# Attention's eight query tiles paired 7,4 / 6,5 / 3,0 / 2,1, with the second tile's masked row copied to free room

## The chip, the cores and the metric

The kernel runs on one core of a Trainium2 chip. The core has five engines with queues of their own: TensorE (PE in the profile; its weight loads are PEld), VectorE (DVE), ScalarE (ACT), GpSimd (POOL) and SyncE (SP), which here only starts DMA transfers. The metric is the device time of one execution in microseconds (us). The kernel before takes 1288.67 us, the median of three runs (1285.36 to 1290.3).

## The reference

One layer with two branches. All of it is computed in float32:

```
h = RMSNorm(x);  h @ w_in -> z_ssm | xBC | dt | q | k | v | f | z_att | g_ssm | g_att
A: causal conv on xBC, SiLU, chunked SSD scan, gated group RMSNorm
B: 16 heads of 64; F = cumsum(log sigmoid(f))
   logits[t, s] = q[t].k[s] / 8 + F[t] - F[s]   for s <= t
   o = softmax(logits) @ v, in blocks of 128 queries;  y_att = o * silu(z_att)
out = (sigmoid(g_ssm) * (A @ w_branch_ssm) + sigmoid(g_att) * (B @ w_branch_att)) @ w_out
x + RMSNorm(out)
```

There are 1024 positions and 1024 channels, so attention has eight query tiles of 128 rows, 0 to 7. Tile i needs the keys 0 to 128(i+1), and only its last 128 keys, the diagonal block, need the causal mask.

## The kernel before, in words

The large products (the projection, both branch products, the last product) run as a stream of matmuls with 512 columns. They are written as fast products of 2x2 blocks, and each operand as a high and a low part, so each step of the stream also needs VectorE and ScalarE work: `sum` (sums of weight blocks), `wop` (high and low part of a weight), `s` and `th` (products taken out of PSUM). `Stream.half()` issues half a step: six matmuls and the work around them.

Attention lies inside this stream. A head pair `hp` (two heads, `e` = 0 and 1) is worked through in six groups; the loop index is m = 6 hp + g. A group is a pair of query tiles against one half `h` of the keys (keys 512 to 1023 are half 1). For each m the order is:

1. `scores` for the pair's first tile (u = 0) and then its second (u = 1): for each head three matmuls into a PSUM tile `s`. VectorE adds the row `fb` (F of the keys, with a large number added on the diagonal block where the mask lies) and takes the minimum in the same operation (L1494), then reads the minimum out into `nm`. ScalarE takes the exponential in place in `ex` and sums it (L1505).
2. `weighted`: the product of the probabilities of the group before with the values, into the PSUM tile `av`.
3. `ahead` halves of the stream (`stream.halves(ahead)`).
4. `loads(m)`: transfers and masks for later groups; then `turned`: TensorE turns `ex` in blocks of 128 x 128 into PSUM tiles `pt` (their buffers are those of `s`, four in all), and ScalarE (L1544), or VectorE for one block of four in the first six head pairs (L1542), copies them to `p`.
5. `behind` halves of the stream.

`room(m)` splits the stream's halves over the groups by the shares in `rooms`; with three halves for a group two go ahead and one behind, with four it is two and two. Operations wrapped in `pin` keep their written order on their engine; the others are placed between them by a planner that plays the program through with its own costs and puts high-priority operations first.

The score rows have these widths (in columns), per head:

| group | tiles, half of the keys | width of u = 0, u = 1 |
|---|---|---|
| 0 | (7,6), 1 | 512, 384 |
| 1 | (7,6), 0 | 512, 512 |
| 2 | (5,4), 1 | 256, 128 |
| 3 | (5,4), 0 | 512, 512 |
| 4 | (3,2), 0 | 512, 384 |
| 5 | (1,0), 0 | 256, 128 |

The mask. `fb` is one row of F, the same on all 128 partitions, and both tiles of a pair read the same 512 columns of it. GpSimd adds `far` (the triangle) to the diagonal block of the first tile in place (`mask(hp, i)`). The second tile's diagonal block must stay unmasked there, because the first tile reads it as ordinary keys. So GpSimd writes the second tile's masked 128 columns to `spare`, the last 128 columns of `ex` at u = 1, which no second tile of a diagonal group uses. The second tile's score row then takes two VectorE operations: the unmasked columns with `fb` (L1494, minimum into `na`), and the diagonal columns with `spare` (L1501), which starts from `na` and gives `nm`. Where the row is only its diagonal block (tiles 4 and 0), it is the second operation alone.

GpSimd runs in written order: the masks, the differences for later products (L211), and transfers it starts itself (L193, L645, L1072, L1575).

## Time and profile before

| | |
|---|---|
| median of three runs | 1288.67 us |
| the profiled execution, its own time | 1288.65 us |
| its span, first to last instruction | 1286.6 us |
| mean granted TensorE clock | 0.994 of full speed |
| TensorE busy | 1246.2 us (97%) |
| VectorE busy | 1015.6 us (79%) |
| ScalarE busy | 790.0 us (61%) |
| GpSimd busy | 329.5 us (26%) |

The profiled execution spends 2.05 us outside the span. Times below are in us from the start of the span. Attention lies between about 680 and 1130. In a row of the timeline the columns are start, duration (of the whole run of instructions, where there are several), engine, line, operation, output and inputs, shape, count, and in square brackets the idle time before it with what ended it. In a row of groups, the numbers after the bar are the busy time in us and the mean of one in ns, and then the idle time of the engine before them. In a row of windows, the columns are the window, its length, the busy time of PE, PEld, DVE, ACT and POOL with instruction counts, the granted clock, the DMA share and GB/s.

### The profile page before, as it was taken

Reading aid. Unit: us, or ns where it says so; the run is one execution under the profiler, and the core shown is the slowest. Engines: PE = TensorE matmul, PEld = TensorE weight load, DVE = VectorE, ACT = ScalarE, POOL = GpSimd, SP = SyncE. Lnnn points to the kernel's source line nnn. Section 1 sums busy time; section 2 is a strip of 40 time slices with the busy share of each in tenths; the row PEclk is TensorE's granted clock in tenths of the full one; section 3 lists DMA queues with packets and bytes.
Section 4 is the critical chain, followed back from the end, with each engine's and each line's share of the span. In section 5 each row is a group of like instructions: output and inputs, shape, how many; then the busy total and the mean of one; then the engine's idle time right before and its main releaser. Section 6 shows DMA issues by size and latency. Waiting matters only on the chain.

```text
span 1286.6 us, 20828 instructions
## 1 busy us (share of the span) xinstructions
PE 1246.2 (97%) x6800; PEld 984.9 (77%) x6800; DVE 1015.6 (79%) x2053; ACT 790.0 (61%) x1719; POOL 329.5 (26%) x384
## 2 busy tenths in 40 slices
PE   5999999999999999999999999999989999999998
PEld 3688888888888888888887777777767776678886
DVE  7999876987789878987667776776779677797975
ACT  7745665566665665576546665667767666743754
POOL 4000440014300340124011322423122222347052
PEclk9999999999999999999999999999989999999999
DMA  8232543545345533653384665576777656756932
GB/s 297 70 123 70 165 147 98 189 156 178 128 147 179 184 126 117 196 180 123 107 290 136 213 213 185 200 239 206 245 284 219 206 196 230 238 185 217 367 113 101
DMA packets 152236, 233.56 MB, mean 182 GB/s; under 512 B 15200, under 2 KB 60736, under 8 KB 152128
## 3 DMA queue, kind: packets, MB, share of 16 engines
q1 hardware_dynamic: 136064, 196.08, 47.3%
q10 hardware_dynamic: 10560, 18.06, 3.7%
q0 software_dynamic: 5504, 18.09, 3.7%
q8 instruction: 53, 0.87, 0.3%
q14 instruction: 55, 0.45, 0.1%
HBM read 162.99 MB, written 72.34 MB: 183 GB/s over the span
## 4 chain that ended last, share of the span: by engine, by line
PE 80%; DVE 8%; DMA 4%; ACT 4%; issue 3%; SPq 1%; POOL 0%; DVEq 0%; ACTq 0%; POOLq 0%
PE pb L128 34%; PE pc L128 20%; PE pd L128 6%; PE pt L131 5%; PE av L128 4%; PE s L128 4%; PE yps L128 2%; DVE wop L351 1%; DMA raw<-in_wu 1%; PE st L128 1%; DVE ex L1494 1%; DMA xt<-in_x 1%; PE tr L131 1%; ACT wop L350 1%; PE tr_v L131 1%
## 5 line engine op out<-in xcount | busy, mean ns | idle before, releaser
L351 DVE TENSOR_TENSOR wop<-sum,wop 128x512 fp32r<-128x512 f32 x180 | 140.6, 783 | 51.5 <-ACT wop L350 50.7
L350 ACT ACTIVATE wop<-sum 128x512 fp32r<-128x512 f32 x180 | 112.3, 626 | 100.9 <-DVE sum L356 48.5
L1505 ACT ACTIVATE ex<-ex,nm 128x512 f32<-128x512 f32 (+1 forms) x192 | 116.7, 608 | 87.6 <-DVE nm L1494 73.1
L410 ACT ACTIVATE s<-pb 128x512 f32<-128x512 f32 x143 | 84.7, 593 | 99.1 <-PE pb L128 97.2
L128 PE MATMUL pb<-x0h,wop 128*128 128x512 f32 x384 | 131.3, 399 | 0.0
L128 PE MATMUL pc<-x3h,wop 128*128 128x512 f32 x384 | 130.8, 398 | 0.4 <-DVE ot L427 0.4
L128 PE MATMUL pc<-x2h,wop 128*128 128x512 f32 x384 | 130.8, 399 | 0.0
L128 PE MATMUL pb<-x4h,wop 128*128 128x512 f32 x384 | 129.2, 395 | 0.0
L128 PE MATMUL pb<-x6h,wop 128*128 128x512 f32 x376 | 127.4, 397 | 1.3 <-ACT s L410 1.3
L128 PE MATMUL pb<-x5h,wop 128*128 128x512 f32 x376 | 127.5, 396 | 0.6 <-ACT s L410 0.6
L351 DVE TENSOR_TENSOR wop<-raw,wop 128x512 fp32r<-128x512 f32 x144 | 105.0, 730 | 26.8 <-ACT wop L350 25.3
L1494 DVE CUSTOM_DVE_ANT_0 ex<-s,fb 128x512 f32<-128x512 f32 (+1 forms) x160 | 86.8, 578 | 21.7 <-PE s L128 19.6
L350 ACT ACTIVATE wop<-raw 128x512 fp32r<-128x512 f32 x144 | 89.6, 623 | 18.2 <-PE pd L128 10.2
L128 PE MATMUL pd<-x1h,wop 128*128 128x512 f32 x288 | 95.8, 392 | 0.0
L131 PE MATMUL pt<-ident,ex 128*128 128x128 f32 x576 | 79.8, 280 | 12.9 <-DVE nm L1501 10.8
L131 PEld LDWEIGHTS pt<-ident,ex 128*128 128x128 f32 x576 | 68.3, 144 | 24.4 <-issue 7.5
L128 PEld LDWEIGHTS pc<-x3h,wop 128*128 128x128 f32 x384 | 72.9, 190 | 17.3 <-issue 1.6
L128 PEld LDWEIGHTS pc<-x2h,wop 128*128 128x128 f32 x384 | 72.5, 189 | 17.8 <-issue 2.4
L128 PEld LDWEIGHTS pb<-x0h,wop 128*128 128x128 f32 x384 | 72.7, 189 | 17.2 <-issue 2.7
L128 PEld LDWEIGHTS pb<-x4h,wop 128*128 128x128 f32 x384 | 72.1, 188 | 16.8 <-issue 2.2
L128 PEld LDWEIGHTS pb<-x5h,wop 128*128 128x128 f32 x376 | 70.6, 188 | 18.4 <-ACT s L410 2.2
L128 PEld LDWEIGHTS pb<-x6h,wop 128*128 128x128 f32 x376 | 71.0, 189 | 17.9 <-ACT s L410 1.7
(314 smaller groups left out, 2975.1 us busy)
## 6 DMA issues: line engine op xcount, KB each, us to landing
raw<-in_wu SPq DMA_DIRECT2D x128, 256.0 KB
csb<-cs_dram SPq DMA_DIRECT2D x32, 256.0 KB
q<-q_dram SPq DMA_DIRECT2D x32, 256.0 KB
k<-k_dram SPq DMA_DIRECT2D x16, 512.0 KB
fb<-f_dram SPq DMA_DIRECT2D x16, 512.0 KB
rb<-st_dram SPq DMA_DIRECT2D x48, 128.0 KB
wd<-in_wo SPq DMA_DIRECT2D x40, 128.0 KB
xt<-in_x SPq DMA_DIRECT2D x8, 512.0 KB
```

Source lines behind the costliest of these rows:

```text
L128: return tc.keep_in_program_order(nc.tensor.matmul(*args, **kw))
L131: return tc.keep_in_program_order(nc.tensor.transpose(out_, in_, idn))
L350: nc.scalar.activation(op[:, 0], src, AF.Copy)
L351: nc.vector.tensor_tensor(op[:, 1], src, op[:, 0], ALU.subtract)
L410: nc.scalar.activation(s, ps, AF.Copy)
L1494: nc.vector.tensor_tensor_reduce(o[:, 0:apart], s[e][:, 0:apart], fb[hp, h][:, e, 0:apart], 1.0, 3.0e38, ALU.add, ALU.min, to,)
L1505: pin(nc.scalar.activation(o, o, AF.Exp, scale=-1.0, bias=nm, accum_out=hd.at(hd.sm, i, h, e)))
```

## The change

The tiles are paired otherwise, and the second tile's whole row, not only its diagonal block, is copied with its mask added.

| group | tiles, half of the keys | width of u = 0, u = 1 |
|---|---|---|
| 0 | (7,4), 1 | 512, 128 |
| 1 | (7,4), 0 | 512, 512 |
| 2 | (6,5), 1 | 384, 256 |
| 3 | (6,5), 0 | 512, 512 |
| 4 | (3,0), 0 | 512, 128 |
| 5 | (2,1), 0 | 384, 256 |

`masked(hp, i)` takes the place of `mask(hp, i, spare)`: GpSimd adds `far` (now 256 columns, of which the first 128 are zeros) to all of the second tile's keys in its diagonal half, 128 columns for tiles 4 and 0, 256 for tiles 5 and 1, and writes them to columns of `ex` at u = 1 behind the tile's own. The score row is then one L1494-like operation for every tile. `q_dram` is laid out by tiles, with the high and the low part of a tile beside each other, so that a pair that isn't adjacent loads in one transfer; each store of `q` then writes four pieces per partition. `weighted` and the last steps of a head pair write and read tiles that aren't adjacent. The shares in `rooms` change; their sum, 6.05, does not.

```diff
-    q_dram = tc.dram_tile([NK, 2, P, T], F32, name="q_dram")
+    q_dram = tc.dram_tile([NK, P, NT, 2, P], F32, name="q_dram")
...
-            nc.scalar.dma_start(dram[i, 0, :, half(ch)], hi)
-            nc.sync.dma_start(dram[i, 1, :, half(ch)], t[ch])
+            for n, (queue, x) in enumerate(((nc.scalar, hi), (nc.sync, t[ch]))):
+                to = place(n, ch)
+                queue.dma_start(to, x if len(to.shape) < 3 else x.rearrange("p (b c) -> p b c", c=P))
...
-            both("q", g, lambda i: parts(q_dram, i, -0.125)),
+            both("q", g, lambda i: parts(lambda n, ch: q_dram[i, :, 4 * ch : 4 * ch + 4, n, :], -0.125)),
...
-        far = ap.tile([P, P], BF16, name="far")
+        far = ap.tile([P, 2 * P], BF16, name="far")
...
-        GROUPS = [((7, 6), 1), ((7, 6), 0), ((5, 4), 1), ((5, 4), 0), ((3, 2), 0), ((1, 0), 0)]
+        GROUPS = [((7, 4), 1), ((7, 4), 0), ((6, 5), 1), ((6, 5), 0), ((3, 0), 0), ((2, 1), 0)]
+        PARTS = ((7, 4), (6, 5))
+        ROOM = {4: 3 * P, 5: 2 * P, 0: P, 1: 2 * P}
+
+        def two(x, pair):
+            return x.rearrange("p (b c) -> p b c", c=P)[:, pair[1] % 4 : pair[0] % 4 + 1 : pair[0] - pair[1]]
...
-            t = ap.tile([P, 2, 256], F32R, tag="q", bufs=2, name="q")
-            cols = slice(pair[1] * P, pair[1] * P + 256)
-            nc.sync.dma_start(t.bitcast(F32), q_dram[hp, :, :, cols].rearrange("n p c -> p n c"))
+            t = ap.tile([P, 2, 2 * P], F32R, tag="q", bufs=2, name="q")
+            src = q_dram[hp].rearrange("p b n c -> p b (n c)")[:, pair[1] : pair[0] + 1 : pair[0] - pair[1]]
+            nc.sync.dma_start(t.bitcast(F32), src)
...
-        spare = ex[:, :, 1, 3 * P : HALF]
-
-        def mask(hp, i, to=None):
-
-            f = diagonal(hp, i)
-            for e in range(2):
-                pin(nc.gpsimd.tensor_tensor((f if to is None else to)[:, e], f[:, e], far, ALU.add))
+        def mask(hp, i):
+
+            f = fb[hp, i // 4][:, :, i % 4 * P : i % 4 * P + P]
+            for e in range(2):
+                pin(nc.gpsimd.tensor_tensor(f[:, e], f[:, e], far[:, P:], ALU.add))
+
+        def apart(i, w):
+            return ex[:, :, 1, ROOM[i] : ROOM[i] + w]
+
+        def masked(hp, i):
+
+            w = (i % 4 + 1) * P
+            for e in range(2):
+                pin(nc.gpsimd.tensor_tensor(apart(i, w)[:, e], fb[hp, i // 4][:, e, 0:w], far[:, 2 * P - w :], ALU.add))
...
-                    o, av = (x.rearrange("p (h c) -> p h c", h=2) for x in (o, av))
-                    z = z.unsqueeze(1).to_broadcast([P, 2, 256])
+                    o, av = (x.rearrange("p (h t c) -> p h t c", h=2, t=2) for x in (o, av))
+                    z = z.unsqueeze(1).to_broadcast([P, 2, 2, P])
...
-            apart = w - P if h == i // 4 and u else w
+            f = apart(i, w) if h == i // 4 and u else fb[hp, h][:, :, 0:w]
...
-                least = 3.0e38
                 with tc.high_priority():
-                    if apart:
-                        to = nm
-                        if apart < w:
-                            least = to = ap.tile([P, 1], F32, tag=f"na{e}", bufs=1, name="na")
-                        pin(
-                            nc.vector.tensor_tensor_reduce(
-                                o[:, 0:apart], s[e][:, 0:apart], fb[hp, h][:, e, 0:apart], 1.0, 3.0e38, ALU.add,
-                                ALU.min, to,
-                            )
+                    pin(
+                        nc.vector.tensor_tensor_reduce(
+                            o, s[e][:, 0:w], f[:, e], 1.0, 3.0e38, ALU.add, ALU.min, nm
                         )
-                    if apart < w:
-                        pin(
-                            nc.vector.tensor_tensor_reduce(
-                                o[:, apart:w], s[e][:, apart:w], spare[:, e], 1.0, least, ALU.add, ALU.min, nm
-                            )
-                        )
+                    )
...
-                bank, first = banks[b], max(b - pair[1], 0)
+                bank, first = banks[b], int(b > pair[1])
...
-            c0 = 256 * h if n < 2 else pair[1] * P
+            to = two(hd.av[n], pair) if n == 2 else two(hd.av[n][:, 256 * h : 256 * h + 256], (1, 0))
             for e in range(2):
                 mm(
-                    hd.av[n][rows[e], c0 + first * P : c0 + 256], v[hp, h][:, b % 4, rows[e]], p[:, e, first:, :],
-                    start=start, stop=stop, skip_group_check=True,
+                    to[rows[e], first:], v[hp, h][:, b % 4, rows[e]], p[:, e, first:, :], start=start, stop=stop,
+                    skip_group_check=True,
                 )
...
             if g in (1, 3, 4):
-                mask(hp, {1: 5, 3: 3, 4: 1}[g])
+                mask(hp, {1: 6, 3: 3, 4: 2}[g])
             if g == 4 and more:
                 mask(hp + 1, 7)
             if g == 4:
-                mask(hp, 0, spare)
+                masked(hp, 1)
             if g == 5 and more:
-                mask(hp + 1, 6, spare)
+                masked(hp + 1, 4)
...
-        rooms = [1.1, 1.1, 0.85, 1.1, 1.05, 0.85]
+        rooms = [0.95, 1.15, 0.95, 1.15, 0.95, 0.9]
...
             made = turned(hp, g, list(end(m - 1)))
             if g in (1, 3):
-                mask(hp, {1: 4, 3: 2}[g], spare)
+                masked(hp, {1: 5, 3: 0}[g])
```

## The prediction

> **What bounds the kernel now.** I read the page first, then the windows, then TensorE's waits, then the timeline at each wait. The page's totals and its chain of waits by engine:

> ```profile
> span 1286.6 us, 20828 instructions
> PE 1246.2 (97%) x6800; PEld 984.9 (77%) x6800; DVE 1015.6 (79%) x2053; ACT 790.0 (61%) x1719; POOL 329.5 (26%) x384
> PE 80%; DVE 8%; DMA 4%; ACT 4%; issue 3%; SPq 1%; POOL 0%; DVEq 0%; ACTq 0%; POOLq 0%
> ```

> TensorE sets the end, so the change is worth what it gives TensorE. By windows (length, PE, PEld, DVE, ACT, POOL, clock, DMA share, GB/s):

> ```profile
> 50.00:600.00 550.00, 548.06 (x2843) 447.52 (x2842) 464.25 (x801) 333.12 (x668) 115.05 (x108) 1.00 0.46 146
> 680.00:1130.00 450.00, 432.92 (x2745) 327.16 (x2744) 334.14 (x922) 298.97 (x748) 122.78 (x207) 0.98 0.65 216
> 1130.00:1200.00 70.00, 70.00 (x314) 57.48 (x313) 59.71 (x73) 30.02 (x54) 39.37 (x25) 1.00 0.68 217
> ```

> TensorE is full before and after attention. In attention it idles 450.0 − 432.9 = 17.1 us, and there the clock is 0.98. TensorE's waits in that window name the cause:

> ```profile
> PE pt L131 <- DVE nm L1501: 10.8, 10, 3.0
> PE pt L131 <- ACT ex L1505: 1.4, 3, 0.7
> ```

> On the timeline all ten of the first kind, and two of the second, stand at the turning of group 0, the pair (7,6) against the later keys: 12.0 us in head pairs 0, 1, 2, 5, 6 and 7. The largest, in pairs 2 and 5:

> ```profile
> 791.16 0.30 PE L131 MATMUL pt<-ident,ex 128*128 128x128 f32 x1 [1.17 <-DVE nm L1501]
> 792.01 1.14 PE L131 MATMUL pt<-ident,ex 128*128 128x128 f32 x5 [0.55 <-DVE nm L1501]
> 952.85 0.44 PE L131 MATMUL pt<-ident,ex 128*128 128x128 f32 x2 [0.65 <-ACT ex L1505]
> 956.26 0.45 PE L131 MATMUL pt<-ident,ex 128*128 128x128 f32 x1 [2.98 <-DVE nm L1501]
> 958.68 1.30 PE L131 MATMUL pt<-ident,ex 128*128 128x128 f32 x5 [1.98 <-DVE nm L1501]
> ```

> The turned blocks need the four PSUM buffers of the scores, so the third cannot start before VectorE is done with the second tile. VectorE in pair 2, and GpSimd beside it:

> ```profile
> 787.97 0.42 DVE L1494 CUSTOM_DVE_ANT_0 ex<-s,fb 128x256 f32<-128x256 f32 x1
> 788.31 1.83 DVE L372 TENSOR_TENSOR sum<-sum,raw 128x512 f32<-128x512 f32 x1
> 790.07 0.68 DVE L1448 TENSOR_TENSOR o<-av,zr 128x512 f32<-128x512 f32 x1
> 790.67 0.34 DVE L1501 CUSTOM_DVE_ANT_0 ex<-s,ex,na 128x128 f32<-128x128 f32 x1
> 788.31 1.29 POOL L211 TENSOR_TENSOR x<-x,th 128x512 f32<-128x512 f32 x1 [1.23 <-DMA th<-ys_dram]
> ```

> The cut in the row is a place where the planner puts other work: from the end of the first part (788.39) to the second part (790.67) two operations that have nothing to do with attention pass. In pair 5 it is the same twice. After the two long stalls the clock falls:

> ```profile
> 792.00:794.00 2.00, 1.99 (x10) 1.69 (x11) 0.69 (x1) 1.89 (x6) 0.00 (x0) 0.55 0.54 182
> 794.00:796.00 2.00, 2.00 (x9) 1.73 (x8) 0.69 (x1) 1.20 (x2) 0.00 (x0) 0.60 0.20 73
> 958.00:960.00 2.00, 1.31 (x7) 1.26 (x8) 1.31 (x5) 1.43 (x4) 0.50 (x1) 0.50 1.05 395
> 960.00:962.00 2.00, 2.00 (x9) 1.90 (x9) 1.78 (x3) 1.75 (x5) 0.00 (x0) 0.50 1.04 413
> ```

> That costs 1.99 × 0.45 + 2.00 × 0.40 = 1.7 us in pair 2, and at least 3.31 × 0.50 = 1.7 us in pair 5.

> **The change, part by part.** The rows that price it:

> ```profile
> L1494 DVE CUSTOM_DVE_ANT_0 ex<-s,fb 128x512 f32<-128x512 f32 x96 | 62.0, 685 | 13.5 <-PE s L128 13.5
> L1494 DVE CUSTOM_DVE_ANT_0 ex<-s,fb 128x256 f32<-128x256 f32 x64 | 25.7, 419 | 8.2 <-PE s L128 6.1 <-POOL fb L1364 2.0
> L1501 DVE CUSTOM_DVE_ANT_0 ex<-s,ex,na 128x128 f32<-128x128 f32 x32 | 11.1, 346 | 2.5
> L1501 DVE CUSTOM_DVE_ANT_0 ex<-s,ex 128x128 f32<-128x128 f32 x32 | 8.4, 285 | 0.5 <-POOL ex L1364 0.4
> L1364 POOL TENSOR_TENSOR ex<-fb,far 128x128 f32<-128x128 f32 x64 | 33.9, 549 | 82.5 <-PE pt L131 63.4 <-DVE nm L1501 11.0 <-ACT p L1544 8.0
> L211 POOL TENSOR_TENSOR x<-x,th 128x512 f32<-128x512 f32 x8 | 10.3, 1290 | 10.0 <-DMA th<-ys_dram 10.0
> L888 POOL TENSOR_TENSOR xe<-xdt,tend 128x256 f32<-128x256 f32 x28 | 25.5, 910 | 200.1 <-DVE xdt L856 195.7 <-PE yps L128 4.3
> L1544 ACT ACTIVATE p<-pt 128x512 f32<-128x512 f32 x104 | 55.6, 588 | 14.7 <-PE pt L131 12.8 <-ACT st L1422 1.1 <-PE pb L128 0.4
> L1544 ACT ACTIVATE p<-pt 128x256 f32<-128x256 f32 x20 | 7.2, 361 | 0.0
> ```

> *VectorE.* Per head and head pair the score rows were 6 of 512 columns, 4 of 256 and 4 of 128; they become 6 of 512, 2 of 384, 2 of 256, 2 of 128. No row has 384; between its neighbours it is (685 + 419) / 2 = 552 ns (419 to 685). So 2 × 419 + 2 × 346 goes and 2 × 552 comes: 0.43 us, × 16 = 6.8 us of VectorE time, and 32 of the pauses between the parts. I credit this only through the stalls.

> *The stalls in group 0.* The second tile there falls from 256 + 128 columns per head, with the pause, to one operation of 128 columns. For both heads that is 2 × (419 + 346 − 285) = 1.0 us less, and the foreign work between the parts (2.3 us in pair 2) has no gap to go into. Cover grows a little too: the product of the group before has 8 full and 4 half matmuls instead of 4 and 4, about 0.4 us by the rows below. So the stalls in pairs 0, 1, 2, 6 and 7 should go (6.4 us of the 12.0). In pair 5 (0.65 + 2.98 + 1.98 = 5.6 us) VectorE is late altogether, busy with operands of the next products, so I leave 2.0 us there, and 0.7 us for the rest: −9.3 us. If nothing but the 1.0 us and the 0.4 us counted, no pair would get back more than 1.4 us: 2 × 1.4 in pairs 2 and 5, and most of the 4.7 us of the other four: about 7.0 us, the lower end. Upper end: all 12.0.

> *The clock.* Pair 2's 1.7 us, and 0.6 of pair 5's 1.7: −2.3 us (0 to −3.4). [...]

> *Products with the values.* Per head pair 64 full and 16 half matmuls become 56 and 32, with the same columns. Full ones, and halves of the same shape elsewhere (`yps`, 64 weights by 128 columns), start to start:

> ```profile
> 859.12 1.95 PE L128 MATMUL av<-p,v 128*64 128x256 f32 x16
> 861.00 0.49 PE L128 MATMUL pb<-x5h,wop 128*128 128x512 f32 x1
> 840.55 0.87 PE L128 MATMUL av<-p,v 128*64 128x256 f32 x8
> 841.35 0.50 PE L128 MATMUL pc<-x2h,wop 128*128 128x512 f32 x1
> 301.06 0.39 PE L128 MATMUL yps<-m,xdt 128*64 128x128 f32 x4
> 301.28 0.39 PE L128 MATMUL yps<-ce,new 128*64 128x128 f32 x4
> ```

> A full one takes 1.88 / 16 = 117 ns, a half 0.22 / 4 = 55 ns: 16 × 55 − 8 × 117 = −0.06 us per head pair. The mixed group of 4 and 4 gives (0.80 − 0.47) / 4 = 83 ns for a half, and +0.4 us per head pair. I take 0; range −0.5 to +3.1 us. The turned blocks stay 72 per head pair.

> *ScalarE.* The copies to `p` go from 12 full and 2 half to 10 and 6: +0.27 us per head pair, 2.1 us in all. ScalarE is busy 299 of 450 us; 0, and 2.1 if that cover were gone.

> *GpSimd.* 32 of the 64 copies to `ex` widen from 128 to 256 columns. No row has this one: between 549 (no more than now) and 1290 ns (the 512 row); I take 0.8 us, near the line between the two, a little under the 910 of the other 256 row. That is +8 us of GpSimd (0 to 24) in 450 us, of which it uses 123. What counts is the moment: the copy for tile 5 is issued behind the turning of group 1, and VectorE in group 2 stops at the second tile until it is there, with every `wop` and `sum` of the stream behind it. TensorE does one half of the stream, the scores, 1.88 us of products and two more halves before it needs the result. A half in the chain of waits:

> ```profile
> 729.65 1.39 PE pc L128 x6
> ```

> Three halves and the products make 3 × 1.4 + 1.9 = 6.1 us, and with the scores about 7, of which VectorE and ScalarE need about 2 for the second tile; two copies take 1.6 to 2.6 us. So it fits, and I put +1.0 us (0 to 3) for copies that come late behind other GpSimd work. The copy for tile 1 is written a whole group ahead.

> *Shares.* By `room`'s own arithmetic both kernels give 156 halves, and two ahead in every group; four to five halves move from the last head pairs to the first. No TensorE work is added: 0.

> *The last group* was 256 and 128 wide, with nothing behind it; now 384 and 256: 2 × 133 + 2 × 134 = 0.5 us of VectorE, and some ScalarE: +0.7 us (0 to 1.5).

> *Stores of q.* The 32 stores cut each partition's 2 KB into four pieces:

> ```profile
> q1 hardware_dynamic: 136064, 196.08, 47.3%
> ```

> At 0.473 × 16 × 1286.6 / 136064 = 72 ns a packet, 32 × 128 × 3 = 12288 more packets would add 55 us over 16 engines at most if small ones cost as much, 1.7 us a store. They fall between 50 and 600, where TensorE is busy 548.06 of 550: 0 (to +1).

> **Sum**, against the profiled execution's own 1288.65 us (span 1286.6; it stands 0.02 below the median): −9.3 − 2.3 + 1.0 + 0.7 = −9.9, so 1278.8; I say 1279.

> **The rivals.** *The stall moves.* Groups 2 and 5 now carry 384 and 256 columns instead of 256 and 128, and group 1 has less cover (its product before is 4 full, 12 half: 1.1 us instead of about 1.7). If the planner fills the time between the first and the second tile as it filled the cut, half of the gain returns as waits in these groups: 1288.65 − 5 = 1284 to 1288. Against it: full groups already live behind the short product of 0.80 us without a stall of note. *The ports.* L372 above lasted 1.83 us, against 0.68 for the next operation of its shape, just while GpSimd's operation of 1.29 us ran. If VectorE's operations on two SBUF inputs wait for each GpSimd operation, up to the whole 8 us is added on VectorE, more than the 6.8 it saves; all of it on the path gives 1279 + 8 = 1287. [...] *Slower: the wide copy is late.* GpSimd works in order and waits for transfers (10.0 us in the L211 row). From about 5 us behind the turning, each further us in groups 2 and 5 is TensorE's; 16 such places with 1.1 us each add 17.6: 1296.6. Against it: VectorE now waits only 2.0 + 0.4 us on GpSimd in the two rows above. *It doesn't do what it says*: the planner puts as much work between the tiles as it did in the cut; that is the first rival's time or the 7.0 us, 1284.

> **How the numbers follow.** A measurement of this kernel tells about 0.5%, 6.4 us, from no change: faster is below 1282.2, slower above 1295.1. The forecast 0.57 (its own range 1273 to 1283), the moved stall (with the change that doesn't do it) 0.20, the ports 0.08, the late copy 0.15. The moved stall reaches below 1282.2 in a small part, so faster 0.58, same 0.27, slower 0.15. Low end: all 12.0 and 3.4 without the added terms, 1273, less 2 for a planner whose order falls well: 1271. High end 1294 leaves the late copy out.

> **What would show it.** Right: the rows L1501 gone, the wait of `pt` on `nm` from 10.8 to about 3 us, PE's idle time in attention from 17 to about 7 to 9, the clock there at 0.99, no window at 0.5 near the third head pair. Wrong: waits of VectorE on GpSimd's `ex` of more than 5 us, waits of `pt` in groups 1, 2 or 5, `av` halves far over 55 ns, or TensorE idle before 600.

## The result, and the profile after

The changed kernel takes 1270.28 us, the median of five runs (1268.43 to 1271.8). Beside it the kernel before takes 1288.39 us (1285.36 to 1290.3). The ratio is 0.986, with a 95% interval of 0.9843 to 0.9878. The change saves 18.1 us where the prediction said 9.9. The direction was right, the size was not, and the time lies just under the low end of the range, 1271 us.

The page of the changed kernel begins like this (totals, then the chain of waits by engine); its profiled execution took 1270.28 us:

```profile
span 1268.6 us, 20886 instructions
PE 1239.5 (98%) x6864; PEld 984.5 (78%) x6864; DVE 1016.4 (80%) x1989; ACT 788.3 (62%) x1735; POOL 331.4 (26%) x384
PE 78%; DVE 8%; DMA 6%; ACT 4%; issue 2%; POOL 0%; SPq 0%; ACTq 0%; DVEq 0%; POOLq 0%
```

VectorE, ScalarE and GpSimd are as busy as before, to within 2 us each, and the span is 18 us shorter. So the gain is not engine time; it is waiting that went away. (Why VectorE's busy time did not fall with its shorter score rows is told under GpSimd's copies.) The windows say where:

```profile
50.00:600.00 550.00, 546.54 (x2836) 446.31 (x2835) 463.52 (x800) 331.82 (x667) 111.66 (x107) 1.00 0.48 146
680.00:1130.00 450.00, 444.76 (x2893) 340.78 (x2892) 351.02 (x881) 306.79 (x780) 134.37 (x212) 1.00 0.67 222
1112.00:1200.00 88.00, 88.00 (x395) 72.19 (x394) 78.52 (x103) 43.95 (x83) 37.93 (x26) 1.00 0.75 258
```

Before attention nothing improved; TensorE is even busy 1.5 us less. Between 680 and 1130 its idle time is 450.0 − 444.8 = 5.2 us, where it was 17.1, and the mean clock there is 1.00 instead of 0.98. TensorE's waits in that window are now:

```profile
PE pt L131 <- DVE nm L1497: 1.3, 4, 0.5
PE s L128 <- DVE p L1538: 1.0, 2, 0.6
PE pt L131 <- ACT ex L1501: 1.0, 3, 0.6
PE pc L128 <- DVE x3l L279: 0.9, 1, 0.9
PE s L128 <- ACT p L1540: 0.6, 2, 0.3
```

(L1497 is the score row, L1501 the exponential, L1538 and L1540 the copies to `p`.) The 10.8 us on `nm` are 1.3. On the timeline none of what is left stands at the turning of group 0, in any head pair: 12.0 us there became 0. VectorE at that place in head pair 2, which held 2.5 us of foreign work in the cut:

```profile
788.73 0.69 DVE L351 TENSOR_TENSOR wop<-raw,wop 128x512 fp32r<-128x512 f32 x1
789.34 0.68 DVE L1497 CUSTOM_DVE_ANT_0 ex<-s,fb 128x512 f32<-128x512 f32 x1
789.95 0.28 DVE L1497 CUSTOM_DVE_ANT_0 ex<-s,ex 128x128 f32<-128x128 f32 x1
790.16 0.28 DVE L1497 CUSTOM_DVE_ANT_0 ex<-s,ex 128x128 f32<-128x128 f32 x1
790.37 0.68 DVE L1456 TENSOR_TENSOR o<-av,zr 128x512 f32<-128x512 f32 x1
```

From the end of the first tile's last row (790.02) to the end of the second tile's last (790.44) 0.42 us pass; before it was 3.81 us. `o`, which stood in the cut, now stands behind it. I call this length the gap below. In the eight head pairs it was 2.58, 2.06, 3.81, 2.07, 2.06, 6.05, 3.04 and 3.63 us; it is 0.42 us in six of them and 1.34 and 1.62 in the two others.

The second part of the gain is the clock. The kernel before had three stretches at half clock in attention: the two that the prediction showed, and one at its end that it missed. By windows of 3.41 us (kernel before):

```profile
792.18:795.59 3.41, 3.41 (x15) 2.91 (x14) 1.38 (x2) 2.90 (x8) 0.00 (x0) 0.50 0.38 132
956.02:959.44 3.42, 1.20 (x5) 0.97 (x6) 3.12 (x10) 1.61 (x6) 1.08 (x2) 0.50 1.05 388
959.44:962.85 3.41, 3.41 (x14) 3.04 (x13) 1.95 (x3) 2.42 (x6) 0.00 (x0) 0.50 0.90 357
1126.69:1130.10 3.41, 3.41 (x8) 2.73 (x9) 3.41 (x7) 1.95 (x5) 0.54 (x1) 0.50 0.31 120
```

Half of the busy time in them is lost, as an estimate: 0.5 × (3.41 + 1.20 + 3.41 + 3.41) = 5.7 us. The changed kernel has no such stretch in attention. So the account is: −12.0 us of idle time at group 0, +0.3 of other idle time (4.5 to 4.75 us on the timeline), −5.7 us of clock; together −17.4 of the span's −18.0.

### The profile page after: what moved, and what is told of

Same layout as the page of the kernel before. It is cut to its first block, busy times and chain, and to the rows that moved or that the text cites. A ratio compares the mean times of both kernels' runs of the same rounds, so it can differ in the third digit from the quotient of the medians.

```text
span 1268.6 us, 20886 instructions
## 1 busy us (share of the span) xinstructions
PE 1239.5 (98%) x6864; PEld 984.5 (78%) x6864; DVE 1016.4 (80%) x1989; ACT 788.3 (62%) x1735; POOL 331.4 (26%) x384
## 3 DMA queue, kind: packets, MB, share of 16 engines
q1 hardware_dynamic: 140160, 196.08, 48.1%
## 4 chain that ended last, share of the span: by engine, by line
PE 78%; DVE 8%; DMA 6%; ACT 4%; issue 2%; POOL 0%; SPq 0%; ACTq 0%; DVEq 0%; POOLq 0%
PE pb L128 33%; PE pc L128 19%; PE pd L128 6%; PE av L128 5%; PE pt L131 5%; PE s L128 4%; PE yps L128 2%; DVE wop L351 1%; DMA xt<-in_x 1%; PE st L128 1%; PE tr L131 1%; DVE sum L356 1%; DVE ex L1497 1%; PE tr_v L131 1%; DVE xs L788 1%
## 5 line engine op out<-in xcount | busy, mean ns | idle before, releaser
L1501 ACT ACTIVATE ex<-ex,nm 128x512 f32<-128x512 f32 (+1 forms) x192 | 116.4, 607 | 75.8 <-DVE nm L1497 74.4
L128 PE MATMUL pb<-x0h,wop 128*128 128x512 f32 x384 | 132.2, 400 | 0.0
L128 PE MATMUL pc<-x3h,wop 128*128 128x512 f32 x384 | 129.8, 396 | 0.6 <-DVE ot L427 0.6
L128 PE MATMUL pc<-x2h,wop 128*128 128x512 f32 x384 | 129.8, 396 | 0.0
L128 PE MATMUL pb<-x4h,wop 128*128 128x512 f32 x384 | 129.2, 395 | 0.0
L128 PE MATMUL pb<-x6h,wop 128*128 128x512 f32 x376 | 126.7, 395 | 1.3 <-ACT s L410 1.3
L128 PE MATMUL pb<-x5h,wop 128*128 128x512 f32 x376 | 126.7, 395 | 0.0
L1497 DVE CUSTOM_DVE_ANT_0 ex<-s,fb 128x512 f32<-128x512 f32 (+1 forms) x128 | 78.6, 653 | 23.2 <-PE s L128 22.8
L128 PE MATMUL pd<-x1h,wop 128*128 128x512 f32 x288 | 95.8, 392 | 0.0
L128 PEld LDWEIGHTS pc<-x3h,wop 128*128 128x128 f32 x384 | 72.1, 188 | 18.0 <-issue 2.4
L128 PEld LDWEIGHTS pb<-x0h,wop 128*128 128x128 f32 x384 | 72.9, 190 | 16.8 <-issue 2.1
L128 PEld LDWEIGHTS pc<-x2h,wop 128*128 128x128 f32 x384 | 72.1, 188 | 17.6 <-issue 2.5
L128 PEld LDWEIGHTS pb<-x4h,wop 128*128 128x128 f32 x384 | 72.1, 188 | 17.3 <-issue 2.5
L128 PEld LDWEIGHTS pb<-x6h,wop 128*128 128x128 f32 x376 | 70.6, 188 | 17.8 <-ACT s L410 1.7
L128 PEld LDWEIGHTS pb<-x5h,wop 128*128 128x128 f32 x376 | 70.6, 188 | 16.4 <-issue 1.6
L211 POOL TENSOR_TENSOR wd<-wd 128x256 f32<-128x256 f32 x32 | 30.2, 944 | 203.0 <-DMA wd<-in_wo 147.1
L131 PE MATMUL pt<-ident,ex 128*128 128x128 f32 x576 | 76.1, 274 | 2.7 <-DVE nm L1497 1.3
```

The source lines that it names most:

```text
L128: return tc.keep_in_program_order(nc.tensor.matmul(*args, **kw))
L131: return tc.keep_in_program_order(nc.tensor.transpose(out_, in_, idn))
L211: pin(nc.gpsimd.tensor_tensor(t[out_], t[a_], t[b_], ALU.subtract))
L1497: nc.vector.tensor_tensor_reduce(o, s[e][:, 0:w], f[:, e], 1.0, 3.0e38, ALU.add, ALU.min, nm)
L1501: pin(nc.scalar.activation(o, o, AF.Exp, scale=-1.0, bias=nm, accum_out=hd.at(hd.sm, i, h, e)))
```

## The experiments

My theory after the comparison: in the kernel before, foreign VectorE work gets between the first tile's score row and `nm` of the second; group 0 has too little cover for it, TensorE stalls, and the stalls halve the clock. The rivals: it is the shares in `rooms`, the layout of `q`, the saved operation in groups 2 and 5, or the narrower second tile of group 0 (128 columns instead of 384), rather than the foreign work. The table sums up each profiled execution: idle time of TensorE from the start of attention to its tail, by the timeline, and the time lost at half clock there.

| kernel | span | idle | clock | span less both |
|---|---|---|---|---|
| before | 1286.6 | 16.5 | 5.7 | 1264.4 |
| changed | 1268.6 | 4.75 | 0 | 1263.9 |
| row cut again in groups 2 and 5 | 1273.8 | 5.9 | 3.1 | 1264.8 |
| before, parts with minima of their own | 1287.2 | 16.6 | 5.8 | 1264.8 |
| changed, old shares | 1269.2 | 6.7 | 0 | 1262.5 |
| before, new shares | 1282.2 | 14.2 | 5.1 | 1262.9 |
| before, new layout of q | 1287.1 | 16.4 | 7.8 | 1262.9 |
| changed, copies twice | 1276.2 | 10.0 | 1.7 | 1264.5 |
| changed, second tile late | 1286.8 | 18.5 | 4.8 | 1263.5 |
| changed, copies to p on ScalarE | 1269.7 | 5.65 | 1.7 | 1262.4 |
| before, cut without pause | 1273.5 | 8.3 | 3.4 | 1261.8 |
| changed, more GpSimd behind | 1270.9 | 7.3 | 1.7 | 1261.9 |

The last column stays within 3 us while the span moves by 18.6: in all twelve kernels, idle time and half clock in attention account for the difference but for these 3 us. What follows asks what makes them.

**One part undone: the row cut again.**

```diff
-            f = apart(i, w) if h == i // 4 and u else fb[hp, h][:, :, 0:w]
+            free = w - P if h == i // 4 and u else w
...
+                    if free < w:
+                        pin(
+                            nc.vector.tensor_tensor_reduce(
+                                o[:, free:w], s[e][:, free:w], apart(i, w)[:, e, free:], 1.0, least, ALU.add, ALU.min,
+                                nm,
+                            )
+                        )
```

> The changed kernel, but tiles 5 and 1 (groups 2 and 5) have their score row cut in two operations again: the unmasked columns with fb, then the 128 diagonal columns, which alone GpSimd copies, starting from the first part's minimum. In group 0 the second tile, 4, is its diagonal block alone and stays one operation. Pairs, shares of the halves and the layout of q are the changed ones. Theory (the 12 us came from group 0, where the narrow tile 4 stands in for the cut row of tile 6; what one operation saves elsewhere is VectorE time under TensorE's work): the changed kernel's 1270 us plus 0 to 3, no idle time of TensorE at the turning of group 0, VectorE's busy time up by about 16 x (2 x 0.35) = 5 to 7 us. Rival (one operation instead of two is what gives): group 2 and 5 get pauses filled with the stream's work, as group 0 had before, and 5 to 9 us come back: 1275 to 1279.

Measured: 1272.87 us (ratio 0.9892, 0.9867 to 0.9918). At the turning of group 0 one wait of 0.15 us is left, in pair 5. The idle time is 1.1 us more than in the changed kernel; the larger part of the difference is one half-clock stretch of 6.8 us at the end of attention:

```profile
1108.66:1112.07 3.41, 1.91 (x10) 1.09 (x10) 2.56 (x13) 2.44 (x8) 0.00 (x0) 1.00 0.84 255
1112.07:1115.48 3.41, 2.86 (x6) 1.97 (x7) 3.38 (x7) 3.41 (x9) 0.54 (x1) 0.50 0.49 187
1115.48:1118.89 3.41, 3.41 (x12) 1.99 (x13) 2.50 (x4) 2.56 (x5) 0.00 (x0) 0.50 0.15 55
```

So the single operation in groups 2 and 5, the only place where the changed kernel has a cut to save, is worth some 3 to 4 us by the medians and the ratios, a little more than the theory said, though the two ratios' intervals overlap. In the profiled execution most of the difference is the half clock; that execution took 1275.56 us, the other three 1272.28 to 1273.0, so this need not hold for them. VectorE's busy time did not rise by the expected 5 to 7 us (1014.4 against 1016.4): its rows for the scores did, by 6.9 us, but its other operations took 8 us less of added time beside GpSimd's (told below).

**The link in the cut.** In the kernel before, the second part of a cut row starts from the first part's minimum.

```diff
-                                o[:, apart:w], s[e][:, apart:w], spare[:, e], 1.0, least, ALU.add, ALU.min, nm
+                                o[:, apart:w], s[e][:, apart:w], spare[:, e], 1.0, 3.0e38, ALU.add, ALU.min, nb
...
+                    if 0 < apart < w:
+                        pin(nc.vector.tensor_tensor(nm, na, nb, ALU.min))
```

> The kernel before with its pairs, but the two parts of a cut row each take a minimum of their own, and a third operation of 128x1 takes the lesser of the two: the second part no longer waits for the first part's result. In the planner's order the two parts then stand right behind each other, and the stream's operations that stood between them come behind the second part or behind the 128x1 operation. Theory (what stalled TensorE is that the result nm comes late, behind foreign VectorE work; the exponentials wait for nm): most of the 12 us of idle time in group 0 stays where foreign work now comes before the 128x1 operation, 1284 to 1290 us; where it comes behind, the stall goes. Rival (it is the cut's own dependence, the second part waiting for the first): the group-0 waits fall under 4 us, and the time to 1278 to 1281.

Measured: 1287.44 us (ratio 1.0001, 0.9987 to 1.0016), so no change. VectorE in pair 2 (L1493 and L1500 are the two parts, L1505 the 128x1 operation):

```profile
789.79 0.29 DVE L1500 CUSTOM_DVE_ANT_0 ex<-s,ex 128x128 f32<-128x128 f32 x1
...
790.00 1.48 DVE L372 TENSOR_TENSOR sum<-sum,raw 128x512 f32<-128x512 f32 x1
791.41 0.68 DVE L1448 TENSOR_TENSOR o<-av,zr 128x512 f32<-128x512 f32 x1
792.01 0.27 DVE L1505 TENSOR_TENSOR nm<-na 128x1 f32<-128x1 f32 x1
```

The two parts now follow each other, and the same two foreign operations have moved behind them, ahead of the 128x1 operation. `nm` is as late as before, and so is TensorE. In both kernels the planner puts its other work right ahead of the operation that needs the result of the one before it.

**The shares alone, both ways.**

```diff
-        rooms = [0.95, 1.15, 0.95, 1.15, 0.95, 0.9]
+        rooms = [1.1, 1.1, 0.85, 1.1, 1.05, 0.85]
```

in the changed kernel, and the reverse in the kernel before.

> The changed kernel with the old shares of the stream's halves (1.1, 1.1, 0.85, 1.1, 1.05, 0.85). Theory (the shares are not what gives): 1270 to 1274 us, no stall at the turning of group 0, perhaps 1 to 3 us of new waits in groups 1, 3 or 5, which have less of the stream now. Rival (the shares carry the gain: with 156 halves in both, they only decide where each one stands): the time goes to 1276 or more, with TensorE idle in groups 1 and 2.

> The kernel before with nothing changed but the shares (0.95, 1.15, 0.95, 1.15, 0.95, 0.9). Theory (the stall is made by the cut row in group 0, not by the shares): 1286 to 1292 us, 9 to 15 us of idle time in attention and the clock at 0.5 in one to four stretches of 3.4 us. Rival (the shares carry the gain): 1270 to 1278 us, and the waits of pt on nm under 3 us.

Measured: 1271.2 us with the old shares in the changed kernel (ratio 0.9872, 0.9843 to 0.9901), and 1283.68 us with the new shares in the kernel before (0.9975, 0.9958 to 0.9992). The shares are worth some 3 us to the kernel before, and nothing that can be told to the changed one. In the kernel before they take the waits at group 0 from 12.0 to 7.4 us, most of it in pairs 2, 5 and 7, and add 2.4 us of waits elsewhere. The cut row still waits:

```profile
PE pt L131 <- DVE nm L1501: 6.6, 7, 2.1
PE pt L131 <- ACT ex L1505: 2.6, 5, 1.1
```

**The layout of q alone.**

```diff
-    q_dram = tc.dram_tile([NK, 2, P, T], F32, name="q_dram")
+    q_dram = tc.dram_tile([NK, P, NT, 2, P], F32, name="q_dram")
```

in the kernel before, with its stores and loads.

> The kernel before with nothing changed but the layout of q: each of the 32 stores cuts a partition's 2 KB in four pieces, and a pair's high and low parts load side by side. Theory (the stores lie under TensorE's work between 50 and 600): 1285 to 1290 us, no idle time of TensorE added before 600. Rival (12288 more packets take room on the queues from the products' operands, or the loads of q come sooner): 1.7 us a store at most, so up to 1290 to 1300, or 1 to 3 us less by the loads.

Measured: 1288.24 us (ratio 1.0006, 0.9992 to 1.002): no change, as the prediction's 0 said. TensorE is busy 547.9 of the 550 us between 50 and 600, against 548.1.

**The pause alone.** This separates what the other runs left together: foreign work in the gap, or the wider tile.

```diff
-                                o[:, apart:w], s[e][:, apart:w], spare[:, e], 1.0, least, ALU.add, ALU.min, nm
+                                o[:, apart:w], s[e][:, apart:w], spare[:, e], 1.0, 3.0e38, ALU.add, ALU.min, nm
```

> The kernel before with its pairs, its shares and its two operations for a cut row, but without the link between them: the diagonal part takes the minimum nm by itself, and the unmasked part's minimum is used by nothing (leaves out: the exponentials of a cut row refer to the minimum of its diagonal part alone, not of the whole row). With no link the order written out for VectorE has 256, 128, 256, 128 columns directly behind each other, with none of the stream's operations between. All widths and all of VectorE's attention work stay as before. Theory (the foreign work that stands in the cut makes the stall; the narrower tile of the new pairs is not needed): from the first tile's last row to the second tile's last about 1.4 us in group 0 instead of 2.1 to 6.1, its waits of pt under 3 us in all, and most of the 18 us come: 1270 to 1276 us. Rival (the narrower second tile gives it, 128 columns instead of 384): 1280 to 1288 us with 6 to 12 us of idle time left in group 0.

Measured: 1274.73 us (ratio 0.9897, 0.988 to 0.9913), the old pairs and widths and 12 us faster than before. VectorE in pair 2:

```profile
784.66 0.42 DVE L1493 CUSTOM_DVE_ANT_0 ex<-s,fb 128x256 f32<-128x256 f32 x1
...
785.01 0.28 DVE L1500 CUSTOM_DVE_ANT_0 ex<-s,ex 128x128 f32<-128x128 f32 x1
...
785.22 0.42 DVE L1493 CUSTOM_DVE_ANT_0 ex<-s,fb 128x256 f32<-128x256 f32 x1
...
785.57 0.28 DVE L1500 CUSTOM_DVE_ANT_0 ex<-s,ex 128x128 f32<-128x128 f32 x1
...
785.78 0.72 DVE L372 TENSOR_TENSOR sum<-sum,raw 128x512 f32<-128x512 f32 x1
```

The gap is 1.11 us (784.74 to 785.85), and TensorE waits at the turning of group 0 in two pairs only: 0.26 us in pair 0 and 3.4 us in pair 5. So with the foreign work out, 384 columns fit under the cover too, but for the 0.26 us of pair 0 and for pair 5, where one foreign operation still stands in a gap of 1.71 us. (Pair 7 has the same gap and no wait.) The largest wait in pair 5 is this one on ScalarE:

```profile
949.75 1.23 PE L131 MATMUL pt<-ident,ex 128*128 128x128 f32 x5 [1.83 <-ACT ex L1504]
```

The two kernels' ratios to before are 0.9897 and 0.986. Of the 18 us, some 12 to 13 need no other pairs. The rest stands in pair 5 and at the tail (a wait of 2.2 us for `x3l` and a half-clock stretch), where this kernel differs from the changed one in widths and shares together; what each of these gives there stays open. A whole masked row for the old pairs was not tried: behind a row of 384 columns `ex` has 128 columns free, not 384.

**VectorE made late.** In the changed kernel, head pairs 0 to 3:

```diff
+            if hp < 4 and g == 0 and u == 1:
+                with tc.high_priority():
+                    for _ in range(3 * hp + 3):
+                        f2 = fb[hp, 1][:, 0, 0 : 2 * P]
+                        pin(nc.vector.tensor_tensor(ex[:, 0, 1, P : 3 * P], f2, f2, ALU.add))
```

> The changed kernel with added VectorE work between the first and the second tile of group 0: 3, 6, 9 and 12 additions of 128x256 in free columns of ex in head pairs 0, 1, 2 and 3, of some 0.4 us each by the 419 ns of the score row of that width, so nm of tile 4 comes 1.3, 2.5, 3.8 and 5.0 us later. The added results are used by nothing. Theory (the turning of group 0 stalls when nm comes later than TensorE's cover, which is 1 to 2 us longer than needed in the changed kernel): no idle time in pair 0, about 1, 2.3 and 3.5 us in pairs 1, 2 and 3, and the clock at half for 3.4 us or more after the stalls of over 1.6 us: 1270 + 6.8 + two or three times 1.7, so 1279 to 1283 us. Rival (VectorE's lateness at this place does not hold TensorE; the gain is VectorE's or TensorE's work elsewhere): 1270 to 1273 us and no waits of pt on nm. [...]

Measured: 1290.2 us (ratio 1.0029, 1.0013 to 1.0044). Work that nothing reads, at this place in four of eight pairs, gives the whole gain back. TensorE at the turning of group 0 in pairs 0 to 3:

```profile
686.11 1.24 PE L131 MATMUL pt<-ident,ex 128*128 128x128 f32 x8 [1.22 <-DVE nm L1502]
743.80 1.54 PE L131 MATMUL pt<-ident,ex 128*128 128x128 f32 x6 [4.03 <-DVE nm L1502]
802.46 1.54 PE L131 MATMUL pt<-ident,ex 128*128 128x128 f32 x6 [3.44 <-DVE nm L1502]
859.68 1.54 PE L131 MATMUL pt<-ident,ex 128*128 128x128 f32 x6 [3.75 <-DVE nm L1502]
```

I had expected 0, 1, 2.3 and 3.5 us. The stalls were larger because each added operation opened a place for foreign work again: in pair 1 six additions (2.5 us) took 4.0 us of it in, and the gap was 6.04 us. Gap less stall gives the cover: 2.38 − 1.22 = 1.2 us in pair 0, and 2.0, 2.9 and 3.5 us in the next three. In the kernel before, the gaps of 2.06 and 2.07 us in pairs 3 and 4 went without a stall, and 3.81 us in pair 2 stalled for 1.7. With each of the three long stalls the clock was at half for 3.41 us, from 743.77, 801.80 and 859.83, as the theory said. The stalls came out 3.4 us long or more, so their length does not show how short a stall suffices. In pair 2 TensorE stops at 799.02 and the half clock begins at 801.80, after 2.8 us.

**GpSimd's copies.** The copies made twice, and, in another kernel, other work of the same amount behind them:

```diff
-            for e in range(2):
+            for e in (0, 1, 0, 1):
```

```diff
+            for n in range(2 * w // P):
+                pin(nc.gpsimd.tensor_tensor(again, fb[hp, i // 4][:, n % 2, w - P : w], far[:, P:], ALU.add))
```

> The changed kernel, but GpSimd makes each copy of a second tile's masked row twice, one pair of copies right behind the other, with the same values: about 23 + 15 = 38 us more of GpSimd, and the row for tile 5 is there 1.5 us later. Theory (the copies are early enough, and VectorE is not held up by GpSimd's operations): 1269 to 1273 us, waits of VectorE on GpSimd's ex under 3 us. Rival of the ports (each of GpSimd's operations holds VectorE up by its own time): up to 38 us more on VectorE, with the slack that TensorE leaves 10 to 25 us more, 1280 to 1295. Rival of the late copy: the 32 wide copies come 1.5 us later, 16 places with 0.5 to 1 us each, 1278 to 1286.

> The changed kernel with more GpSimd work behind the copies of a second tile's row, not ahead of them: two or four additions of 128x128 into a tile that nothing reads (in a shorter number type, by lack of room), 96 in all, about 47 us of GpSimd by the 475 to 515 ns of its rows of that shape. The rows themselves are there as early as in the changed kernel. It tells apart the two things in the run with the copies made twice, which was 6 to 7 us longer: if that came from rows that were late, this one takes 1270 to 1272 us; if it came from GpSimd's operations lengthening VectorE's at the same time, VectorE's busy time is again 5 to 9 us over the 1016 us of the changed kernel, and the time 1275 to 1279 us.

Measured: 1277.16 us (ratio 0.9923, 0.9905 to 0.9941) and 1273.73 us (0.9896, 0.9877 to 0.9915). The waits of VectorE on GpSimd with the copies made twice, and the row that the second kernel adds to GpSimd:

```profile
DVE ex L1497 <- POOL ex L1372: 2.5, 4, 1.8
```

```profile
L1375 POOL TENSOR_TENSOR again<-fb,far 128x128 bf16<-128x128 f32 x94 | 52.4, 558 | 4.9
```

GpSimd is busy 376.5 us with the copies made twice and 386.5 us in the second kernel, where the changed kernel has 331.4; VectorE is busy 1023.7, 1011.1 and 1016.4 us. So GpSimd's time is not simply added to VectorE's. But the totals hide what happens to single operations. Here are GpSimd's copies for the last group of pair 4 in the changed kernel, VectorE's operations at that time, and TensorE just behind them:

```profile
939.13 2.21 POOL L1372 TENSOR_TENSOR ex<-fb,far 128x256 f32<-128x256 f32 x2
939.65 2.24 DVE L279 TENSOR_TENSOR x5l<-x5l,x5h 128x512 fp32r<-128x512 f32 x2
942.29 0.96 PE L131 MATMUL pt<-ident,ex 128*128 128x128 f32 x5 [0.51 <-DVE nm L1497]
```

Two such VectorE operations take 1.29 us with no copy beside them (the row at 948.48 further down). So it is throughout the traces of the kernel before, the changed one and these two. Of VectorE's operations that run while GpSimd is idle, none takes over 0.02 us more than the median of its kind (operation, shape and tiles). Of those that run beside a GpSimd operation, 148 to 172 in each trace take 0.07 to 3.7 us more. All of these read SBUF alone; no score row, and nothing else that reads PSUM, is among them. The added time is 73 us in the kernel before, 80 in the changed one, 88 with the copies made twice and 75 in the second kernel. Without it VectorE is busy 942, 937, 936 and 936 us.

So VectorE's operations do take longer beside GpSimd's here, as the rival that the prediction calls the ports supposed; by what mechanism, no run shows. From before to after, the score rows take 6.8 us less and this added time is 6.6 us more, which is why VectorE's busy time did not fall. The 7.3 us of VectorE with the copies made twice are such added time too. How much of it reaches TensorE is not shown as a whole. At the place above, VectorE's rows would by these durations have ended 0.95 us sooner, before TensorE's wait of 0.51 us began, so that wait is likely its price.

The lateness of the rows does not explain the 7 us of the first kernel: behind VectorE's wait of 1.8 us for `ex`, at 999, TensorE does not wait before 1053. In the profiled executions TensorE's idle time and half clock rise by 6.9 us with the copies made twice and by 4.3 us in the second kernel. The largest wait of both is new, 1.81 and 1.55 us at the turning of group 1 in the last pair, where VectorE's rows come later. Why they do stays open, and so do the 3 us of the second kernel, which fit neither expectation.

**A try at the rest.**

```diff
-                    if b % 4 == 1 and hp < NK - 2:
+                    if b % 4 == 1 and hp < NK - 4:
```

> The changed kernel, but in head pairs 4 and 5 too all copies to p go to ScalarE (VectorE makes one in four only in pairs 0 to 3). VectorE is busy without a break between about 935 and 980, where 2.2 of the changed kernel's 4.75 us of idle time of TensorE lie; 18 copies of some 0.6 us go to ScalarE. Theory: 1 to 2 us of these 2.2 go, 1268 to 1270 us, within what can be told from the changed kernel. Rival (ScalarE's exponentials come late instead): 1270 to 1275 us, waits of pt on ScalarE's ex in pairs 4 and 5.

Measured: 1270.44 us (ratio 0.9872, 0.9853 to 0.9891), no better than the changed kernel. Its idle time is 5.65 us. The two waits at 944 to 946 were 0.85 and 0.62 us, where the changed kernel had 0.51 and 0.16, and they cost a half-clock stretch. No version tried beats the changed kernel.

## Why the prediction was right or wrong

The mechanism was right. What failed is the size of two terms, the stalls and the clock, both put too low; two smaller costs did not come.

**The bound and the place: right.** TensorE was the bound, the stalls at the turning of group 0 were what the change removed, and the foreign work in the cut made them. The run with the pause alone taken out shows the last point directly: 3.65 us of the 12.0 are left there.

**The stalls in group 0, −9.3 us: mis-sized, measured −12.0.** The failed step is "VectorE is late altogether" in pair 5, for which I left 2.0 us. The changed kernel has no wait there. VectorE was not late altogether; eight foreign operations (5.4 us) had been placed ahead of `nm`. In the changed kernel the same place holds two:

```profile
948.48 1.29 DVE L279 TENSOR_TENSOR x3l<-x3l,x3h 128x512 fp32r<-128x512 f32 x2
949.69 0.28 DVE L1497 CUSTOM_DVE_ANT_0 ex<-s,ex 128x128 f32<-128x128 f32 x1
```

What VectorE's load there does cost is some 2 us spread over other groups between 935 and 980. The lower end of 7.0 us, made from 1.0 us of width and 0.4 us of cover per pair, rested on the wrong quantity: the gap fell by 1.6 to 4.4 us per pair but for one of 0.7, and the width makes 0.7 of that (1.11 us with the pause alone taken out, 0.42 in the changed kernel). The rest is the foreign work and the link. But VectorE's load in pair 5 does count with the old widths: with the pause alone taken out, 3.4 us of stalls stay there, 1.83 of them behind ScalarE. What takes these away in the changed kernel, widths or shares, stays open.

**The clock, −2.3 us: the term most off, measured −5.7.** Three errors have one sign. I counted only part of pair 5, which is 2.3 us in full and not "at least" 1.7. I credited 0.6 of it because of the stall I had left there. And I did not look for half clock outside group 0; the stretch at 1126.69, worth 1.7 us, follows the wait for `x3l` at the tail. In the changed kernel that wait is 0.86 us instead of 1.56 and leaves the clock alone. No term of the prediction stood for this last part, so it was luck. A stretch near that place came back in the runs with the cut restored and with the pause taken out; the other five runs with the new pairs have none there.

**Products, ScalarE, shares, stores of q, at 0: right**, as far as the runs tell, but for one reservation on the shares. For the products with the values the rows now are

```profile
L128 PE MATMUL av<-p,v 128*64 128x256 f32 x440 | 57.9, 390 | 0.0
L128 PE MATMUL av<-p,v 128*64 128x128 f32 x252 | 19.0, 273 | 0.0
```

76.9 us, against 77.2 in the same two rows of before (65.2 and 12.0). The shares and the stores have runs of their own above. The shares give nothing that can be told in the changed kernel; to the kernel before they were worth some 3 us, for which the reason given (no TensorE work is added) had no room. The packets of two queues rose, q1 from 136064 by 4096 and q10 from 10560 by 6144:

```profile
q1 hardware_dynamic: 140160, 196.08, 48.1%
q10 hardware_dynamic: 16704, 18.06, 4.0%
```

That is 10240 in all, near the 12288 worked out. The rest fits the loads of q: those of an adjacent pair, 16 of 32, now need one piece per partition and not two, 2048 packets less. With the layout alone, where all 32 pairs are adjacent, q1 rose by 2048 and q10 by 6144, 4096 less than 12288.

**Late copies, +1.0 us: not there.** The copy was priced well and came in time:

```profile
L1372 POOL TENSOR_TENSOR ex<-fb,far 128x256 f32<-128x256 f32 x32 | 23.2, 746 | 32.4 <-PE pt L131 32.4
L1497 DVE CUSTOM_DVE_ANT_0 ex<-s,ex 128x256 f32<-128x256 f32 x32 | 12.3, 417 | 0.8 <-POOL ex L1372 0.8
```

746 ns against my 0.8 us, and VectorE waits 0.8 us in all, none of which reaches TensorE. Making the copies twice shows that there is margin: one of them came 1.8 us late, and TensorE did not wait for it. What the copies do cost is time of VectorE's other operations while they run, as told above.

**The last group, +0.7 us: not seen.** The waits from group 5's scores to the tail fell from 3.0 us (1.13, 0.15, 0.20, 1.56) to 2.0 (0.26, 0.25, 0.61, 0.86).

So the 8.1 us by which the span's 18.0 exceed the forecast's 9.9 are 2.7 for the stalls, 3.4 for the clock and 1.7 for two costs that did not come, less 0.3 for other waits; 0.6 us is left without a name.

**The rivals.** The moved stall came, but small: the waits of `pt` in groups other than 0 rose from 0.5 to 2.3 us, other waits fell by 1.5, and together idle time outside group 0 rose by 0.3 us. What the rival of the ports supposed, for which one row of 1.83 us spoke, came true on VectorE, where 6.6 us more of added time beside GpSimd's operations took back the 6.8 us that the score rows saved; the time of 1287 did not come, since TensorE's idle time in attention is 4.75 us in all. Every VectorE operation that took over 0.02 us longer than the median of its kind, in the four traces counted above, ran beside a GpSimd operation; the 148 in the kernel before and 151 in the changed one that took 0.07 us or more longer read SBUF alone. The late copy and the change that doesn't do what it says did not happen.

**The signs.** All that would show it right came, and went further: `pt` on `nm` at 1.3 us (about 3), idle time 5.2 us (7 to 9), clock 1.00 (0.99). Of the signs for wrong, only short waits of `pt` in other groups came, 0.6 us at the most and 2.3 us together.

## What to carry to other kernels

Look at what stands, in the order as it is run, between the last input and the result that another engine waits for: a chain of two operations is a place where a planner puts foreign work, and taking the link away was worth some 12 us here with no operation saved. Add to the stalls of TensorE the half clock that may follow them (5.7 us beside 16.5 us of idle time in the kernel before), and search the whole span for half-clock stretches before costing a change. Where a stall is put down to an engine that is "busy", count how much of that work really has to come first. And when work moves to GpSimd, look at the durations of VectorE's operations beside it (6.6 us more here), operation by operation: a total can stay the same while rows that got shorter pay for others that got longer.

## What the runs showed of the hardware that was not expected

```profile
788.77:792.18 3.41, 1.69 (x10) 1.11 (x9) 2.95 (x8) 1.36 (x6) 2.24 (x4) 1.00 0.66 199
983.33:986.74 3.41, 2.27 (x16) 1.33 (x16) 3.41 (x9) 1.74 (x5) 1.07 (x2) 1.00 0.68 246
986.74:990.15 3.41, 3.41 (x21) 2.90 (x20) 3.16 (x12) 2.85 (x8) 0.00 (x0) 1.00 0.80 236
```

```profile
954.79:958.20 3.41, 1.72 (x14) 1.49 (x15) 3.38 (x9) 3.41 (x10) 0.00 (x0) 1.00 0.92 302
958.20:961.61 3.41, 3.41 (x21) 2.64 (x21) 3.34 (x7) 3.08 (x8) 2.57 (x5) 1.00 0.99 368
```

With 1.72 us idle the next window ran at half clock (shown above); with 1.14 us it did not, nor did it with 1.69 us in the second kernel. In attention in both kernels and in seven runs (all but the row cut again, the parts with minima of their own and the old shares), with idle time as the timeline gives it, every window at full clock with 1.72 us or more of idle time was followed by half clock and none with 1.25 us or less; between 1.28 us (new shares, followed) and the 1.69 us above both occur, so what decides there stays open. Of the windows that are at half clock themselves, those with 2.20 us of idle time (kernel before, at 956.04) and 1.56 us (new layout of `q`, at 957.67) were followed by half clock again, and so was one with 0.55 us where the row was cut again (at 1112.07 above), while one with 0.66 us (second tile late, at 801.80) was not. Idle time of 1.49 us inside one window cost 1.7 us more, half of 3.41, with the new layout of `q` (the window at 790.47), and nothing more with parts with minima of their own (at 790.37).
